# Two operand sums moved ahead of a subtraction, and a 144-column short product, in a two-layer decoder trunk

## The chip, the cores and the metric

The kernel runs on one core of a Trainium2 chip. The metric is the device time of one execution in microseconds; less is better. Five engines work side by side, each through its own queue of instructions: TensorE (PE, with its weight loads PEld), VectorE (DVE), ScalarE (ACT), GpSimd (POOL) and SyncE (SP). Here POOL and SP only start transfers.

## The reference

The program computes two layers of a decoder trunk on 512 tokens of width 1024 in float32. Each layer adds three sub-layers to its input, and each of them is normalised before and after:

```python
for l in range(DEPTH):                     # DEPTH = 2
    h = rms_norm(x, gn[0])
    x = x + 0.5 * rms_norm(swiglu(h, w_ffn1_gate[l], w_ffn1_up[l], w_ffn1_down[l]), gn[1])
    h = rms_norm(x, gn[2])
    ...                                    # recurrence, windowed attention, two gated branches
    x = x + rms_norm(mixed @ w_out[l], gn[3])
    h = rms_norm(x, gn[4])
    x = x + 0.5 * rms_norm(swiglu(h, w_ffn2_gate[l], w_ffn2_up[l], w_ffn2_down[l]), gn[5])
```

`swiglu` is `(silu(h @ w_gate) * (h @ w_up)) @ w_down` with an inner width of 2816, that is 22 blocks of 128 columns. Four of these feed-forward stages and two mixers (the middle sub-layer) make the program.

## The kernel before

**Products from halves.** TensorE multiplies numbers of reduced precision (fp32r). So that the result has the precision of float32, every operand is split into a high half `hi` (a cast) and a low half `lo` (the rest), and `mm3` issues three matmuls for each product of two blocks: hi·hi, hi·lo and lo·hi.

**The stream of weights.** The class `Stream` loads weights from `wall` into tiles `w32` (4 buffers), and `split` turns them into pairs `whi` and `wlo` (6 buffers each). What is split next, and when its instructions are written, is set by `ahead` (line 373), which `used` calls whenever TensorE's instructions for a block have been written. The instructions for TensorE stand in the order in which the program writes them; those for the other engines are placed by a scheduler, except for those that `pin` or `hold` keep in the order of the program.

**A pair of weights.** Most of a feed-forward stage's gate and up products are made by `sevenths` (line 1036), which makes the four quarters of one output block from seven smaller products instead of eight. It takes a pair of weight tiles u and u+1 and needs four stationary operands of it, which `split` makes in the order a, b, c, d:

- a is the tile u itself, d the second half of the tile u+1. Their low halves are made by a transfer: ACT writes −w, rounded, into `wlo` (line 355), ACT casts `whi` (line 359), and POOL starts a DMA that adds w to what stands in `wlo` (line 358).
- b is the sum `t13` (lines 340 and 341, on DVE), c the sum `t`, which takes `t13` further (lines 347 and 348 before the change). Their `whi` is a cast on ACT (line 359), their `wlo` a subtraction on DVE (line 363), which reads that cast.

Between the making of b's sums and its low half stands `self.product()`, which places the last step of the previous output block, the product of gate and up (`gate`, line 1087). That step needs ACT's silu (line 1084), which needs the sums of the seven products (lines 1063, 1065, 1069 and 1070, on DVE). The sums have two buffers (tag `tt`), which the row of gains `grow` (line 733) and the tiles `mv` of the recurrence (line 1183) share.

In one pair TensorE makes 84 matmuls of 256 columns: 7 products of 4 blocks of 3 matmuls. The first feed-forward stage has 15 pairs, the other three have 19 each; each mixer has 4 pairs, and there `split` does not pin its work.

**After the pairs** comes `down` (line 700): the product with `w_down`, in matmuls of 512 columns. Its first part, `both(j, 0)`, takes whole blocks; then `quarters` (line 950) makes seven products from quarters, whose operands (`Late`, line 649; `quarter`, line 258) are made by ACT, DVE and POOL while the first part runs. After the first of the seven products ACT copies two results out (line 978).

**Short products.** `lead` (line 1032) is a matmul of only a few columns into a place that the next matmul overwrites; its result is not used. It stands at the head of the pairs of a stage, with 144 columns, and in `quad` (line 995), where the first products of a stage run over the two halves of the tokens one after the other: ahead of the third product of each half, with 112 columns. Five `quad` calls run in halves, so there are ten of these.

Of the kernel before, what the change touches and what calls it, by code (L numbers as in the profile page):

```python
# [7 lines left out]
F32 = mybir.dt.float32  # L8
# [3 lines left out]
ALU = mybir.AluOpType  # L12
# [3 lines left out]
P = 128  # L16
D = 1024
# [20 lines left out]
TURN = 0  # L38
SEVEN = 16
ASIDE = 16  # L40
LEAD, LEAD_IN = 144, 112
ORDER = ("p1", "p3", "p7", "p2", "p6", "p5")
HEADS = (0, 4, 1, 5, 2, 6, 3, 7)

# [2 lines left out]
def trunk(ctx: ExitStack, tc: tile.TileContext, xin, wall, gains, lbT, hgain, sinks, c_dist, c_mask, c_ident, out):  # L47
    nc = tc.nc
    cp = ctx.enter_context(tc.tile_pool(name="cp", bufs=1))
    sb = ctx.enter_context(tc.tile_pool(name="sb", bufs=1))  # L50
# [9 lines left out]
    def nm(s):  # L60
        seq[0] += 1
        return f"{s}_{seq[0]}"
# [7 lines left out]
    def acc():  # L70
        return ps.tile([P, S], F32, tag="acc", name=nm("acc"), bufs=5)
# [43 lines left out]
    def mm(o, lhsT, rhs, start, stop):  # L115
        nc.tensor.matmul(o, lhsT, rhs, start=start, stop=stop)  # L116
        n = 1
        for d in rhs.shape[1:]:
            n *= d
        if rhs.dtype == F32:  # L120
            order.t += max(n / 2.4, 27.0) * (2 if lhsT.shape[1] == 64 and n < 256 else 4)
        else:
            order.t += max(n / 2.4, 107.0)
# [24 lines left out]
    pin = tc.keep_in_program_order  # L148
# [10 lines left out]
    class Stream:  # L159
# [164 lines left out]
        def split(self):  # L324
            it = self.items[self.done]
            if it.kind[0] == "p":
                return self.quarter(it)
            u, last = it.u, it.kind in "uvd"
            self.load(u + (1 if it.kind in "uv" else 2))
            it.hi, it.lo = (sb.tile([P, D + 64], F32R, tag=t, name=nm(t), bufs=WS)[:, it.at : it.at + D] for t in ("whi", "wlo"))  # L330
            w, h = self.raw[u], (slice(0, D // 2), slice(D // 2, D))
            cols = (slice(0, D),)
            if it.kind == "u" and u < 2:
                cols = h
            if it.kind in "bcd":
                v = self.raw[u + 1]
            if it.kind == "b":

                self.t13 = sb.tile([P, D], F32, tag="tt", name=nm("tt"), bufs=2)
                pin(nc.vector.tensor_tensor(self.t13[:, h[0]], w[:, h[0]], v[:, h[0]], op=ALU.add))  # L340
                pin(nc.vector.tensor_tensor(self.t13[:, h[1]], v[:, h[0]], v[:, h[1]], op=ALU.add))
                w = self.t13
                self.product()
            elif it.kind == "c":

                t = sb.tile([P, D], F32, tag="tt", name=nm("tt"), bufs=2)
                pin(nc.vector.tensor_tensor(t[:, h[0]], self.t13[:, h[0]], v[:, h[1]], op=ALU.add))
                pin(nc.vector.tensor_tensor(t[:, h[1]], t[:, h[0]], w[:, h[1]], op=ALU.add))  # L348
                w = t
            elif it.kind == "d":  # L350
                w = v
                cols = h[1:]
            for c in cols:
                if it.kind in "vad":
                    i = nc.scalar.mul(it.lo[:, c], w[:, c], -1.0)  # L355
                    if self.pinned or self.tight:
                        pin(i)
                    nc.gpsimd.dma_start(it.lo[:, c].bitcast(F32), w[:, c], accum_op=ALU.add)  # L358
                i = nc.scalar.copy(it.hi[:, c], w[:, c])  # L359
                if u < 6 or self.pinned or self.tight:  # L360
                    pin(i)
                if it.kind not in "vad":
                    self.hold(nc.vector.tensor_tensor(it.lo[:, c], w[:, c], it.hi[:, c].bitcast(F32), op=ALU.subtract))  # L363
            self.done += 1
            self.flight += 1
            if last:
                nu = u + (1 if it.kind in "uv" else 2)
                for i in range(u, nu):
                    self.raw.pop(i)
                    self.freed += 1  # L370
                self.load(self.freed + W32)
# [46 lines left out]
    def wmm(o, b, mv, start, stop, poll=True):  # L418

        mm3(o, b[2:], mv, start, stop)  # L420
        ws.used(b)
        if poll:
            order.poll()

    def cut(pair, c):
        return pair[0][:, c], pair[1][:, c]
# [73 lines left out]
    def pair_split(v, how=split):  # L500
        return how(v, to=(big(F32R, [P, 2, S // 2]), big(F32R, [P, 2, S // 2])))
# [13 lines left out]
    class First(Quarters):  # L515
# [44 lines left out]
        def sums(self):  # L560

            k = len(self.x56)
            a = []
            for i in range(2):
                f = xs[k + 4 * i]
                nc.vector.scalar_tensor_tensor(f, f, g_sb[:, 0, 0, k + 4 * i : k + 4 * i + 1], self.rb, op0=ALU.mult, op1=ALU.mult)
                a.append([f[:, c] for c in HALF])
            self.x124.append([])
            for v in (a[0][0], a[1][0], a[1][1]):
                x = big(F32R, [P, 2, S // 2])  # L570
                split(v, to=(x[:, 0, :], x[:, 1, :]))
                self.x124[k].append(x)
            for x, v in zip((self.x56, self.x37), quarter_sums(a[0][0], a[1][0], a[0][1], a[1][1])):
                x.append(pair_split(v))
# [74 lines left out]
    class Late:  # L649
# [20 lines left out]
        def first(self, k):  # L670
            x = big(F32R, [P, 2, S // 2])
            self.x1.append(split(self.src[k][:, HALF[0]], to=(x[:, 0, :], x[:, 1, :]), hold=pin))
# [322 lines left out]
    def quad(pre, halves):  # L995

        o = [acc() for _ in range(4)]
        blocks = {}
        ws.pinned = halves
        for half in (0, 1) if halves else (None,):  # L1000
            c = WHOLE if half is None else HALF[half]
            for k in range(KT):
                order.until(lambda: pre.have[half or 0] > k)
                for j in range(4):
                    if (k, j) not in blocks:
                        blocks[k, j] = ws.next(uses=2 if halves else 1)
                    if halves and (k, j) == (0, 2):
                        lead(o[j][:, c], blocks[k, j][2], pre.h[k][0][:, c], LEAD_IN)
                    wmm(o[j][:, c], blocks[k, j], cut(pre.h[k], c), k == 0, k == KT - 1)
            ws.pinned = False  # L1010
        return o
# [20 lines left out]
    def lead(o, st, mv, n):  # L1032

        mm(o[:, :n], st, mv[:, :n], True, True)
# [60 lines left out]
    def ffn(l, n, pre, nxt, halves=True):  # L1095
        a = []

        def gated(og, ou):
            z, u = big(), big()
            if first:  # L1100
                pin(nc.vector.tensor_tensor(z, og, pre.rb, op=ALU.mult))
                nc.scalar.activation(out=z, in_=z, func=AF.Silu)
                nc.vector.tensor_tensor(u, ou, pre.rb, op=ALU.mult)
                nc.vector.tensor_tensor(u, u, z, op=ALU.mult)
            else:
                nc.scalar.activation(out=z, in_=og, func=AF.Silu)
                pin(nc.vector.tensor_tensor(u, ou, z, op=ALU.mult))
            a.append(u)

        first = isinstance(pre, First)  # L1110
        o = quad(pre, halves)
        if first:
            o.append(project(pre))
            o.append(project(pre, aux))
            order.until(lambda: pre.rb is not None)
        if not first:
            pre.sums()
            pre.sums()
        for j in range(2):
            gated(o[2 * j], o[2 * j + 1])  # L1120
        if first:
            gated(o[4], o[5])
            for j in range(3, FIRST):
                if j > 3:
                    order.until(lambda: pre.laid)
                    pre.sums()
                if j == 4:
                    pre.sums()
                if j == FIRST - 1:
                    ws.most = AHEAD + 2  # L1130
                gated(project(pre), project(pre))
            fast(pre, a, FIRST)
        else:
            pre.sums()
            ws.most = AHEAD + 2
            og = project(pre)
            pre.sums()
            gated(og, project(pre))
            fast(pre, a, 3)
        return down(a, FT, l, n + 1, nxt, True)  # L1140
# [125 lines left out]
    def mixer(l, pre, nxt):  # L1266
# [40 lines left out]
        def run(i, heads):  # L1307
# [8 lines left out]
            for n in range(2):  # L1316
                order.spawn(outputs(i + n, box[n]), n * WAIT["apart"])

        o = quad(pre, True)
        order.spawn(run(0, [head(o[2 * i], o[2 * i + 1], i) for i in range(2)]))  # L1320

# [176 lines left out]
    pre = First()  # L1498
# [68 lines left out]
    for l in range(DEPTH):  # L1567
        pre = ffn(l, 0, pre, (l, 2), halves=l > 0)
        pre = mixer(l, pre, (l, 4))
        pre = ffn(l, 4, pre, (l + 1, 0) if l + 1 < DEPTH else None)  # L1570
# [81 lines left out]
```

## Time and profile before

| what | value |
|---|---|
| time, median of 3 runs | 2051.83 us (2051.58 to 2052.47) |
| span of the profiled execution | 2051.3 us |
| PE busy | 2032.0 us |
| DVE busy | 1623.7 us |
| ACT busy | 1249.4 us |
| POOL busy | 268.3 us |
| read from and written to memory | 213.43 MB and 14.73 MB |

The profiled execution is one execution; its span, from the first to the last instruction, is 0.5 us under the median of the times. A share of busy time is an average over stages. Matmuls are pipelined, so PE counts as busy from a matmul's start to its modelled end, and two neighbours overlap; how fast they follow each other is read from their starts, or from their number in a window.

### The profile page before, as it was taken

Reading aid. Unit: us, or ns where it says so; the run is one execution under the profiler, and the core shown is the slowest. Engines: PE = TensorE matmul, PEld = TensorE weight load, DVE = VectorE, ACT = ScalarE, POOL = GpSimd, SP = SyncE. Lnnn points to the kernel's source line nnn. Section 1 sums busy time; section 2 is a strip of 40 time slices with the busy share of each in tenths; the row PEclk is TensorE's granted clock in tenths of the full one; section 3 lists DMA queues with packets and bytes.
Section 4 is the critical chain, followed back from the end, with each engine's and each line's share of the span. In section 5 each row is a group of like instructions: output and inputs, shape, how many; then the busy total and the mean of one; then the engine's idle time right before and its main releaser. Section 6 shows DMA issues by size and latency. Waiting matters only on the chain. (4 is left out here: it accounts for less than half of the span.)

```text
span 2051.3 us, 36423 instructions
## 1 busy us (share of the span) xinstructions
PE 2032.0 (99%) x13553; PEld 1815.3 (88%) x13553; DVE 1623.7 (79%) x2894; ACT 1249.4 (61%) x2213; POOL 268.3 (13%) x318
## 2 busy tenths in 40 slices
PE   9999999999999999999999999999999999999998
PEld 8899878877888999997899998888778989999987
DVE  5887889767676778888988878987686858788888
ACT  7556687446355556657866566874554545665684
POOL 0111140000000011113201111400000100111140
PEclk9999999999999999999999999999999999999999
DMA  8577788312237357778757778872122553777694
GB/s 257 152 194 186 189 187 238 117 65 70 73 94 215 113 146 192 190 188 205 200 157 191 193 186 203 179 230 92 62 73 62 137 194 102 182 190 194 175 201 123
DMA packets 166801, 328.07 MB, mean 160 GB/s; under 512 B 19072, under 2 KB 85088, under 8 KB 166624
## 3 DMA queue, kind: packets, MB, share of 16 engines
q1 hardware_dynamic: 122416, 228.16, 33.5%
q0 software_dynamic: 44064, 97.54, 27.3%
q8 instruction: 106, 1.74, 0.4%
q14 instruction: 71, 0.58, 0.1%
q10 hardware_dynamic: 144, 0.05, 0.0%
HBM read 213.43 MB, written 14.73 MB: 111 GB/s over the span
## 5 line engine op out<-in xcount | busy, mean ns | idle before, releaser
L116 PE MATMUL acc<-s,whi 128*128 128x256 f32 (+1 forms) x4998 | 1023.7, 304 | 0.3 <-ACT whi L359 0.3
L116 PEld LDWEIGHTS acc<-s,whi 128*128 128x128 f32 x4998 | 793.6, 188 | 47.0 <-issue 3.2
L116 PE MATMUL acc<-s,wlo 128*128 128x256 f32 (+1 forms) x2488 | 755.3, 304 | 5.3 <-DMA wlo<-w 5.2
L116 PEld LDWEIGHTS acc<-s,wlo 128*128 128x128 f32 x2488 | 467.9, 188 | 30.6 <-DMA wlo<-w 7.4
L116 PE MATMUL acc<-whi,s 128*128 128x512 f32 x1360 | 443.9, 394 | 4.9 <-ACT whi L288 3.6
L359 ACT CAST whi<-w 128x1024 fp32r<-128x1024 f32 (+1 forms) x310 | 284.8, 926 | 144.9 <-PE acc L116 103.5
L359 ACT CAST whi<-tt 128x1024 fp32r<-128x1024 f32 x160 | 168.1, 1051 | 250.5 <-DVE tt L348 192.3
L358 POOL DMA_DIRECT2D wlo<-w x178 | 154.7, 870 | 1232.8 <-ACT wlo L355 987.0
L116 PEld LDWEIGHTS acc<-whi,s 128*128 128x128 f32 x1360 | 255.8, 188 | 64.3 <-ACT whi L288 4.8
L363 DVE TENSOR_TENSOR wlo<-tt,whi 128x1024 fp32r<-128x1024 f32 x160 | 196.1, 1225 | 131.4 <-ACT whi L359 129.1
L116 PE MATMUL acc<-wlo,s 128*128 128x512 f32 x680 | 267.3, 393 | 1.8 <-DVE wlo L296 1.6
L116 PE MATMUL aux<-s,whi 128*128 128x256 f32 (+1 forms) x1296 | 228.5, 279 | 0.0
L363 DVE TENSOR_TENSOR wlo<-w,whi 128x1024 fp32r<-128x1024 f32 (+1 forms) x132 | 157.4, 1206 | 74.2 <-ACT whi L359 73.9
L116 PEld LDWEIGHTS aux<-s,whi 128*128 128x128 f32 x1296 | 196.6, 188 | 1.1 <-issue 0.5
L116 PE MATMUL aux<-s,wlo 128*128 128x256 f32 (+1 forms) x648 | 180.4, 278 | 0.0
L116 PEld LDWEIGHTS acc<-wlo,s 128*128 128x128 f32 x680 | 128.2, 188 | 32.1 <-DVE wlo L296 7.5
L355 ACT ACTIVATE wlo<-w 128x1024 fp32r<-128x1024 f32 (+1 forms) x178 | 153.1, 862 | 2.6 <-DMA w<-wall 1.9
L116 PE MATMUL aux<-whi,s 128*128 128x512 f32 x432 | 143.9, 390 | 0.0
L444 POOL DMA_DIRECT2D s<-s x128 | 111.1, 972 | 219.1 <-ACT s L432 100.2
L116 PEld LDWEIGHTS aux<-s,wlo 128*128 128x128 f32 x648 | 121.7, 188 | 0.3
L296 DVE TENSOR_TENSOR wlo<-s,whi 128x512 fp32r<-128x512 f32 x160 | 102.7, 686 | 9.9 <-ACT whi L288 8.1
L432 ACT CAST s<-s 128x512 fp32r<-128x512 f32 (+1 forms) x140 | 70.8, 548 | 44.8 <-DVE s L491 39.3
(184 smaller groups left out, 2466.9 us busy)
## 6 DMA issues: line engine op xcount, KB each, us to landing
w<-wall SPq DMA_DIRECT2D x267, 512.0 KB, 3.7
wlo<-w POOLq DMA_DIRECT2D x98, 512.0 KB, 5.1
w<-wall SPq DMA_DIRECT2D x224, 128.0 KB, 3.5
wlo<-w POOLq DMA_DIRECT2D x80, 256.0 KB, 3.3
s<-wall SPq DMA_DIRECT2D x128, 128.0 KB, 4.3
s<-s POOLq DMA_DIRECT2D x64, 256.0 KB, 5.0
x_d<-s SPq DMA_DIRECT2D x48, 256.0 KB, 4.6
s<-x_d SPq DMA_DIRECT2D x48, 256.0 KB, 5.1
```

Source lines behind the costliest of these rows:

```text
L116: nc.tensor.matmul(o, lhsT, rhs, start=start, stop=stop)
L296: pin(nc.vector.tensor_tensor(it.lo[:, h[c]], w[c], it.hi[:, h[c]].bitcast(F32), op=ALU.subtract))
L355: i = nc.scalar.mul(it.lo[:, c], w[:, c], -1.0)
L358: nc.gpsimd.dma_start(it.lo[:, c].bitcast(F32), w[:, c], accum_op=ALU.add)
L359: i = nc.scalar.copy(it.hi[:, c], w[:, c])
L363: self.hold(nc.vector.tensor_tensor(it.lo[:, c], w[:, c], it.hi[:, c].bitcast(F32), op=ALU.subtract))
L432: (hold or ws.hold)(nc.scalar.copy(hi, src))
L444: nc.gpsimd.dma_start(lo.bitcast(F32), src, accum_op=ALU.add)
```

## The change

Two things change. In `split`, the sum `t`, the operand of c, is made in the step of b: its first half directly after `t13`, then `self.product()`, then its second half, all ahead of b's low half. The step of c only takes the finished tile. The same instructions are issued, in another order. In `quad`, the short product has 112 columns in the first half of the tokens, as before, and 144 in the second.

```diff
-LEAD, LEAD_IN = 144, 112
+LEAD, LEAD_IN = 144, (112, 144)
...
                 pin(nc.vector.tensor_tensor(self.t13[:, h[0]], w[:, h[0]], v[:, h[0]], op=ALU.add))
                 pin(nc.vector.tensor_tensor(self.t13[:, h[1]], v[:, h[0]], v[:, h[1]], op=ALU.add))
+                self.t = t = sb.tile([P, D], F32, tag="tt", name=nm("tt"), bufs=2)
+                pin(nc.vector.tensor_tensor(t[:, h[0]], self.t13[:, h[0]], v[:, h[1]], op=ALU.add))
+                self.product()
+                pin(nc.vector.tensor_tensor(t[:, h[1]], t[:, h[0]], w[:, h[1]], op=ALU.add))
                 w = self.t13
-                self.product()
             elif it.kind == "c":
 
-                t = sb.tile([P, D], F32, tag="tt", name=nm("tt"), bufs=2)
-                pin(nc.vector.tensor_tensor(t[:, h[0]], self.t13[:, h[0]], v[:, h[1]], op=ALU.add))
-                pin(nc.vector.tensor_tensor(t[:, h[1]], t[:, h[0]], w[:, h[1]], op=ALU.add))
-                w = t
+                w = self.t
...
-                        lead(o[j][:, c], blocks[k, j][2], pre.h[k][0][:, c], LEAD_IN)
+                        lead(o[j][:, c], blocks[k, j][2], pre.h[k][0][:, c], LEAD_IN[half])
```

The first place is DVE in a pair of a feed-forward stage. In the rows before, `tt_1049` is `t13` and `tt_1082` is `t`; the two rows that write `wlo` are the low halves of b and of c.

```order
L1070 TENSOR_TENSOR m_1002<-aux_921,s_923 128x512
L340 TENSOR_TENSOR tt_1049<-w_175_847,w_176_849 128x512
L341 TENSOR_TENSOR tt_1049<-w_176_849 128x512
L1087 SCALAR_TENSOR_TENSOR s_1036<-m_1002 128x512
L363 TENSOR_TENSOR wlo_1048<-tt_1049,whi_1047 128x1024
L347 TENSOR_TENSOR tt_1082<-tt_1049,w_176_849 128x512
L348 TENSOR_TENSOR tt_1082<-tt_1082,w_175_847 128x512
L363 TENSOR_TENSOR wlo_1081<-tt_1082,whi_1080 128x1024
L1063 TENSOR_TENSOR m_1129<-acc_1039,s_1042 128x2x256
```

The same place after the change, where `tt_1052` is `t`, and its two sums have the lines 343 and 345.

```order
L1070 TENSOR_TENSOR m_1002<-aux_924,s_926 128x512
L340 TENSOR_TENSOR tt_1049<-w_175_847,w_176_849 128x512
L341 TENSOR_TENSOR tt_1049<-w_176_849 128x512
L343 TENSOR_TENSOR tt_1052<-tt_1049,w_176_849 128x512
L1087 SCALAR_TENSOR_TENSOR s_1036<-m_1002 128x512
L345 TENSOR_TENSOR tt_1052<-tt_1052,w_175_847 128x512
L363 TENSOR_TENSOR wlo_1048<-tt_1049,whi_1047 128x1024
L363 TENSOR_TENSOR wlo_1084<-tt_1052,whi_1083 128x1024
L1063 TENSOR_TENSOR m_1129<-acc_1039,s_1042 128x2x256
```

Both sums of `t` now stand ahead of the low half of b, one on each side of the gate product (line 1087), and the two low halves stand side by side. ACT's order within such a pair is the same before and after.

The second place is ACT ahead of the first pair of the first mixer, where nothing is pinned. Before, `whi_6429` is c of the first pair, `whi_6463` its d, `whi_6516` and `wlo_6517` are a of the second pair, and `whi_6485` is a weight of a branch.

```order
L432 CAST s_6399<-s_6393 128x512
L432 CAST s_6403<-s_6394 128x512
L432 CAST s_6419<-aux_6414 128x512
L1439 ACTIVATE s_6448<-acc_6407 128x512
L1051 COPY s_6479<-acc_6475 128x256
L359 CAST whi_6429<-tt_6431 128x1024
L359 CAST whi_6463<-w_1083_6087 128x512
L355 ACTIVATE wlo_6464<-w_1083_6087 128x512
L359 CAST whi_6485<-w_1096_6157 128x1024
L359 CAST whi_6516<-w_1118_6239 128x1024
L355 ACTIVATE wlo_6517<-w_1118_6239 128x1024
```

After the change c of the first pair is `whi_6432`; the other names of weights are the same.

```order
L359 CAST whi_6432<-tt_6362 128x1024
L359 CAST whi_6463<-w_1083_6087 128x512
L359 CAST whi_6485<-w_1096_6157 128x1024
L355 ACTIVATE wlo_6464<-w_1083_6087 128x512
L359 CAST whi_6516<-w_1118_6239 128x1024
L432 CAST s_6402<-s_6396 128x512
L355 ACTIVATE wlo_6517<-w_1118_6239 128x1024
L432 CAST s_6406<-s_6397 128x512
L359 CAST whi_6545<-tt_6547 128x1024
L432 CAST s_6422<-aux_6417 128x512
L1439 ACTIVATE s_6448<-acc_6410 128x512
L1051 COPY s_6479<-acc_6475 128x256
```

The work on the weights has moved ahead of the splits of the activations (line 432), of the gate of a branch (line 1439) and of the copy of the first product (line 1051).

On PE only the five short products in the second half change, from 128x112 to 128x144; every other row stands where it stood. On SP the load of the row of gains (line 734) stands one load of weights later in four of its six places, and POOL's order is the same.

## The prediction

> **What bounds the kernel now.** I read the page first, then the waits of PE, then where those waits lie.
>
> ```profile
> PE 2032.0 (99%) x13553; PEld 1815.3 (88%) x13553; DVE 1623.7 (79%) x2894; ACT 1249.4 (61%) x2213; POOL 268.3 (13%) x318
> PE acc L116 <- DMA wlo<-w: 5.2, 8, 1.2
> PE acc L116 <- ACT whi L288: 3.6, 3, 1.6
> ```
>
> PE sets the end. Its two largest waits, for low halves that come by DMA and for high halves in `down`, make 8.8 us, 0.4% of the span. If that were all, little could be won. But a busy PE need not run at its best, so I look at lengths: for the four feed-forward stages in order, the short product that opens the pairs, the first matmul of 512 columns after them, and the copy of the first of the seven products in `down`. The columns are start, duration, instruction.
>
> ```profile
> 88.20 0.51 PE L116 MATMUL acc<-s,whi 128*128 128x144 f32 x3
> 231.12 0.40 PE L116 MATMUL acc<-whi,s 128*128 128x512 f32 x1
> 265.74 1.05 ACT L978 COPY s<-acc 128x512 f32<-128x512 f32 x2
> ...
> 728.74 0.39 PE L116 MATMUL acc<-s,whi 128*128 128x144 f32 x2
> 913.55 0.40 PE L116 MATMUL acc<-whi,s 128*128 128x512 f32 x1
> 947.25 1.06 ACT L978 COPY s<-acc 128x512 f32<-128x512 f32 x2
> ...
> 1062.97 0.51 PE L116 MATMUL acc<-s,whi 128*128 128x144 f32 x3
> 1246.28 0.40 PE L116 MATMUL acc<-whi,s 128*128 128x512 f32 x1
> 1281.47 1.05 ACT L978 COPY s<-acc 128x512 f32<-128x512 f32 x2
> ...
> 1742.11 0.39 PE L116 MATMUL acc<-s,whi 128*128 128x144 f32 x2
> 1929.76 0.40 PE L116 MATMUL acc<-whi,s 128*128 128x512 f32 x1
> 1960.57 1.06 ACT L978 COPY s<-acc 128x512 f32<-128x512 f32 x2
> ```
>
> The first stage takes 231.12 − 88.20 = 142.92 us for 15 pairs, 9.53 us each. The others have 19 pairs, and at that pace would take 181.03. They take 184.81, 183.31 and 187.65: 3.8, 2.3 and 6.6 us more. From the end of the pairs to the copy the four stages take 34.62, 33.70, 35.19 and 30.81 us for the same instructions: the last is 3.8, 2.9 and 4.4 us quicker than the others.
>
> Next, what runs beside PE in a pair: DVE from one L1063 to the next, ACT, and PE's wait there. The bracket holds the idle time before an instruction and what ended it.
>
> ```profile
> 1114.15 0.68 DVE L1063 TENSOR_TENSOR m<-acc,s 128x512 f32<-128x512 f32 x1
> ...
> 1117.13 0.68 DVE L341 TENSOR_TENSOR tt<-w 128x512 f32<-128x512 f32 x1
> 1117.73 0.68 DVE L1087 SCALAR_TENSOR_TENSOR s<-m 128x512 f32<-128x512 f32 x1
> 1118.99 1.23 DVE L363 TENSOR_TENSOR wlo<-tt,whi 128x1024 fp32r<-128x1024 f32 x1 [0.57 <-ACT whi L359]
> 1120.13 0.69 DVE L347 TENSOR_TENSOR tt<-tt,w 128x512 f32<-128x512 f32 x1
> 1120.85 0.69 DVE L348 TENSOR_TENSOR tt<-tt,w 128x512 f32<-128x512 f32 x1
> 1122.71 1.23 DVE L363 TENSOR_TENSOR wlo<-tt,whi 128x1024 fp32r<-128x1024 f32 x1 [1.17 <-ACT whi L359]
> 1123.85 0.69 DVE L1063 TENSOR_TENSOR m<-acc,s 128x512 f32<-128x512 f32 x1
> 1117.90 1.05 ACT L359 CAST whi<-tt 128x1024 fp32r<-128x1024 f32 x1 [0.56 <-DVE tt L341]
> 1121.63 1.05 ACT L359 CAST whi<-tt 128x1024 fp32r<-128x1024 f32 x1 [2.41 <-DVE tt L348]
> 1122.58 0.63 ACT L355 ACTIVATE wlo<-w 128x512 fp32r<-128x512 f32 x1
> 1121.40 0.38 PE L116 MATMUL acc<-s,wlo 128*128 128x256 f32 x1 [0.80 <-DMA wlo<-w]
> ```
>
> DVE's period is 1123.85 − 1114.15 = 9.70 us, more than the 9.53 of PE, and L1063 waits for nothing: DVE and ACT hand work to each other in a loop slower than PE. DVE is late for want of a partner, since 0.57 + 1.17 = 1.74 us of its period are waits for ACT, while ACT waits 2.41 for L348. Behind that cast stand the −w of d and a and their transfers. So each pair loses 0.17 us of lead, 3.2 over 19 pairs; late in a stage PE waits for a transfer, and enters `down` with DVE and ACT behind. The last stage is the control: its PE takes 187.65 / 19 = 9.88 us a pair, longer than the loop, so the loop gained lead, and its `down` is the quick one.
>
> Why was PE slow there? The window rows give length, then PE's busy time with its number of matmuls, PEld, DVE, ACT and POOL, the granted clock and DMA.
>
> ```profile
> 1063.00:1120.00 57.00, 57.00 (x505) 57.00 (x504) 45.23 (x64) 35.10 (x49) 10.33 (x12) 1.00 0.76 183
> 1772.00:1929.00 157.00, 157.00 (x1335) 157.00 (x1335) 127.04 (x177) 97.71 (x134) 26.66 (x31) 1.00 0.77 192
> 1771.60 0.39 PE L116 MATMUL acc<-s,wlo 128*128 128x256 f32 x1 [0.41 <-DMA wlo<-w]
> ```
>
> 57.00 / 505 is 112.9 ns a matmul, 157.00 / 1335 is 117.6, with the clock at 1.00 in both. PE has two paces for the same matmuls; the slow one began at the one wait of that stage and held to its end.
>
> **The sums of c ahead of b's low half.** Nothing is added or taken away in instructions; two DVE sums of 0.72 us (from one start to the next) move ahead of a subtraction of 1.14. After L341 DVE goes on for 0.72 + 0.60 + 0.72 us (L343, L1087, L345), to 1119.77, which covers b's cast on ACT (1117.90 to 1118.95). c's cast runs while DVE makes b's low half. Both waits, 1.74 us, lose their cause, and the loop becomes 9.70 − 1.74 = 7.96 us. ACT's busy share, 35.10 / 57.00, gives 5.97 us a pair; with DVE at 7.96 and PE at 9.53, PE is the slowest, and DVE and ACT will wait for it. c's cast, and all of ACT behind it, starts about 0.1 us after L345's end at 1119.77, that is 1.75 us sooner in each pair until buffers stop it.
>
> Behind the moved sums stands b's low half. It starts at 1119.77 instead of 1118.99, 0.78 later, and ends near 1120.9. PE reads it 24 matmuls after the start of the group whose third matmul is the row of 1121.40: 22 × 0.113 = 2.5 us later, at 1123.9. The delay costs nothing while that cover of 3 us lasts. The gate product, one sum later by 0.72, feeds only `down`.
>
> What this gives, against the profiled execution:
> - Pairs: the three stages fall to the first one's pace, 3.8 + 2.3 + 6.6 = 12.7 us. This counts the waits and the slow pace of the last stage, which needs the wait to begin. Bounds: 12.7, and 6.4 if the last stage stays as slow as it is (1335 matmuls × 4.7 ns = 6.3 us).
> - Entry to `down`: the three slower stages fall to the last one's length, 3.8 + 2.9 + 4.4 = 11.1. Bounds: 11.1, and 0 if DVE's own work there is what is late. I take the upper end because the last stage has the same work and only a better lead.
> - Mixer: unpinned, so its order changes.
>
> ```profile
> 588.22 1.05 ACT L359 CAST whi<-tt 128x1024 fp32r<-128x1024 f32 x1
> 592.10 1.06 ACT L355 ACTIVATE wlo<-w 128x1024 fp32r<-128x1024 f32 x1
> 603.11 0.38 PE L116 MATMUL acc<-s,wlo 128*128 128x256 f32 x1 [1.22 <-DMA wlo<-w]
> ```
>
> The −w of the second pair's a, at 592.10, now stands ahead of four small steps and of c's former place at 588.22. 1.2 us sooner is enough to end the wait of 1.22. Bounds: +1.2, and −1.2 if the steps now behind the casts (line 432) come late for PE; I take 1.2, since no row names PE waiting for line 432 there.
>
> The load of the gains' row stands one load later in SP's queue; it is read only after the seven products, so I cost it at nothing.
>
> One part of the 4.4 us is a clock.
>
> ```profile
> 1272.97 0.50 PE L116 MATMUL acc<-whi,s 128*128 128x512 f32 x1 [1.59 <-ACT whi L288]
> 1274.10:1277.50 3.40, 3.40 (x9) 2.60 (x8) 3.37 (x9) 1.31 (x3) 0.86 (x1) 0.50 1.03 257
> ```
>
> After a wait of 1.59 us the granted clock was 0.50 for 3.40 us, a loss of 1.7. I count it as going with the wait. The Trainium skill (TensorE: Matmul & The Clock Gate, "What's actually happening") says that the clock halves after an idle window of some 3.4 us; by that the wait was too short to be the cause, and the sum would be 1.7 us less. Here the trace speaks against it, as PE was not idle that long.
>
> **The short product.** Five times, 32 more columns: by the pace above 14 ns each, 0.07 us together. What it may move is the pace behind it.
>
> ```profile
> L116 PE MATMUL acc<-s,whi 128*128 128x256 f32 x44 | 7.7, 276 | 0.0
> 360.96 0.51 PE L116 MATMUL acc<-s,whi 128*128 128x112 f32 x3
> L116 PE MATMUL acc<-s,whi 128*128 128x256 f32 x59 | 10.6, 282 | 0.0
> ```
>
> The groups are of 88.6 to 98.6 us, behind the 144 columns at 88.20, and of 361.3 to 371.4, behind the 112 columns of a second half. A matmul's mean is 276 ns at the quick pace and 282 at the slow. If 144 columns bring the quick pace here too, the 59 matmuls of this group and half as many with the low half, 88 × 4.7 ns × 5 = 2.0 us are won; if not, 0.07 lost. The 144 row comes behind 512 columns, not 256, so it is no sure guide: I take the middle, 1.0.
>
> **Sum.** 12.7 + 11.1 + 1.2 + 1.0 = 26.0 us, against the span 2051.3; the median lies 0.5 above the span, so 2051.8 − 26.0 = 2025.8.
>
> **The rivals.**
> 1. *The pace turns.* The waits go, but one stage of pairs runs at 117.6 ns: 19 × 84 × 4.7 ns = 7.5 us, hence about 2033. For it: the last stage shows that a stage can stay slow to its end. Against: the first runs all its 15 pairs quick. Chance 0.19.
> 2. *`down` is late by itself.* Only the pairs, the mixer and the short product give: 2051.8 − 14.9 = 2036.9. Against: the last stage. Chance 0.10.
> 3. *The transfers don't come sooner*, because POOL starts them later as DVE's gaps close; PE still waits for low halves, and the time stays near 2051. Against it:
>
> ```profile
> L358 POOL DMA_DIRECT2D wlo<-w x37 | 31.9, 861 | 162.2 <-ACT wlo L355 160.8 <-ACT whi L359 1.3
> 1123.51 0.86 POOL L358 DMA_DIRECT2D wlo<-w  x1 [6.71 <-ACT wlo L355]
> ```
>
> The start at 1123.51 ran beside the L363 of 1122.71 and took 0.86, like the mean of 37. The Trainium skill (GPSIMD Engine Reference, "Specifications") says that GpSimd contends with VectorE's instructions of two SBUF inputs, which all these sums are; the row shows none. Chance 0.04.
> 4. *Slower: the loop gets longer.* L1087 now stands between the sums of c and waits for ACT's silu; were silu late, L345, c's cast and, through ACT's queue, the next silu would all be late. It decides from a period of 9.70 us, that is when new waits exceed the 1.74 removed; at 10.0 it costs 0.3 × 72 pairs = 22 us, 2073. Against: L341 and L343 give ACT 1.3 us for a silu that now makes L1087 wait for nothing. Chance 0.03.
>
> The forecast has 0.64. The range 2021 to 2037 holds it and rivals 1 and 2. Its lower end is the whole 2.0 of the short product and some 4 us of PE's smaller waits, which a better lead may end: of the 19.3 us between span and PE's busy time 10.5 are left beside the 8.8 above. Differences under 0.2% (4.1 us) can't be told from none: faster 0.93 (the forecast, 1 and 2), same 0.04 (3), slower 0.03 (4).
>
> **What would show it.** Right: the two L363 of a pair side by side with hardly a wait; L1063 or L1070 waiting for PE; no PE wait for `wlo` in the pairs; 181 us from short product to 512 columns in the three stages; about 31 us from there to the copy in all four; 276 ns in the second halves. Wrong: a stage with 281 ns, a `down` still over 33 us to the copy, or L363 still behind ACT.

## The result, and the profile after

| what | before | after |
|---|---|---|
| time, median of 4 runs | 2052.15 us (2051.58 to 2052.83) | 2024.78 us (2024.60 to 2024.90) |
| span of the profiled execution | 2051.3 us | 2023.0 us |

The ratio is 0.9868, with a 95% interval from 0.9854 to 0.9882: faster by 1.3%. The forecast was 2025.8. The medians differ by 27.4 us and the spans by 28.3; the profiled execution after took 2024.79 us. From the page of the changed kernel, the busy times; then its waits of PE, with the total, the number and the longest.

```profile
PE 2016.2 (100%) x13553; PEld 1809.1 (89%) x13553; DVE 1624.3 (80%) x2894; ACT 1265.2 (63%) x2213; POOL 268.3 (13%) x318
```

```profile
PE aux L116 <- DVE eps_t L139: 1.1, 1, 1.1
PE acc L126 <- DVE s L863: 1.0, 2, 0.5
PE acc L116 <- DVE wlo L296: 0.2, 1, 0.2
```

The waits for `wlo` by DMA (5.2 us) and for `whi` of L288 (3.6) are gone; three small ones are left, and PE is busy for 2016.2 of 2023.0 us. The three landmarks of each stage, as before: the short product, the first matmul of 512 columns, the first copy in `down`.

```profile
88.27 0.51 PE L116 MATMUL acc<-s,whi 128*128 128x144 f32 x3
231.19 0.40 PE L116 MATMUL acc<-whi,s 128*128 128x512 f32 x1
261.31 1.06 ACT L978 COPY s<-acc 128x512 f32<-128x512 f32 x2
...
722.02 0.51 PE L116 MATMUL acc<-s,whi 128*128 128x144 f32 x3
903.02 0.40 PE L116 MATMUL acc<-whi,s 128*128 128x512 f32 x1
933.15 1.05 ACT L978 COPY s<-acc 128x512 f32<-128x512 f32 x2
...
1048.93 0.51 PE L116 MATMUL acc<-s,whi 128*128 128x144 f32 x3
1229.93 0.40 PE L116 MATMUL acc<-whi,s 128*128 128x512 f32 x1
1260.05 1.06 ACT L978 COPY s<-acc 128x512 f32<-128x512 f32 x2
...
1720.81 0.39 PE L116 MATMUL acc<-s,whi 128*128 128x144 f32 x2
1901.81 0.40 PE L116 MATMUL acc<-whi,s 128*128 128x512 f32 x1
1931.93 1.06 ACT L978 COPY s<-acc 128x512 f32<-128x512 f32 x2
```

The differences account for most of the gain in the span:

| stretch | stage 1 | stage 2 | stage 3 | stage 4 | won |
|---|---|---|---|---|---|
| pairs, before | 142.92 | 184.81 | 183.31 | 187.65 | |
| pairs, after | 142.92 | 181.00 | 181.00 | 181.00 | 12.8 |
| from there to the copy, before | 34.62 | 33.70 | 35.19 | 30.81 | |
| from there to the copy, after | 30.12 | 30.13 | 30.12 | 30.12 | 13.8 |

That is 26.6 of the 28.3 us. From the first stage's copy to the second stage's pairs, where the first mixer lies, it is 463.00 before and 460.71 after, 2.3 us less; the other stretches differ by 0.1 to 0.3 us, and their sum is 0.6 us longer.

A pair after the change, on DVE, from one pair of low halves (L363, two in one row) to the next; the bracket holds the idle time and what ended it.

```profile
1109.99 2.48 DVE L363 TENSOR_TENSOR wlo<-tt,whi 128x1024 fp32r<-128x1024 f32 x2
1113.17 0.69 DVE L1063 TENSOR_TENSOR m<-acc,s 128x512 f32<-128x512 f32 x1 [0.70 <-PE acc L116]
...
1115.89 0.69 DVE L1070 TENSOR_TENSOR m<-aux,s 128x512 f32<-128x512 f32 x1 [0.85 <-PE aux L116]
...
1117.70 0.69 DVE L343 TENSOR_TENSOR tt<-tt,w 128x512 f32<-128x512 f32 x1
1118.30 0.69 DVE L1087 SCALAR_TENSOR_TENSOR s<-m 128x512 f32<-128x512 f32 x1
1118.90 0.69 DVE L345 TENSOR_TENSOR tt<-tt,w 128x512 f32<-128x512 f32 x1
1119.51 2.48 DVE L363 TENSOR_TENSOR wlo<-tt,whi 128x1024 fp32r<-128x1024 f32 x2
```

The two low halves stand side by side and neither waits for ACT. DVE's period is 9.52 us, and 0.70 + 0.85 = 1.55 of it are waits for PE, where before it waited 1.74 for ACT. By these brackets DVE itself needs 9.52 − 1.55 = 7.97. L1087, now between the sums, waits for nothing here. Over all pairs the pages tell the same; before, then after, with the idle time behind the second bar:

```profile
L363 DVE TENSOR_TENSOR wlo<-tt,whi 128x1024 fp32r<-128x1024 f32 x160 | 196.1, 1225 | 131.4 <-ACT whi L359 129.1
L363 DVE TENSOR_TENSOR wlo<-tt,whi 128x1024 fp32r<-128x1024 f32 x160 | 195.4, 1221 | 9.9 <-ACT whi L359 7.3
```

ACT beside the pair after the change:

```profile
1110.16 1.05 ACT L359 CAST whi<-tt 128x1024 fp32r<-128x1024 f32 x1 [0.49 <-DVE tt L345]
1111.81 0.63 ACT L355 ACTIVATE wlo<-w 128x512 fp32r<-128x512 f32 x1 [0.60 <-PE acc L116]
1114.53 1.06 ACT L355 ACTIVATE wlo<-w 128x1024 fp32r<-128x1024 f32 x1 [1.58 <-PE aux L116]
```

The cast of c waits 0.49 us for its sum where it waited 2.41, and the two −w (L355) wait until PE has let go of a buffer. So the loop is ahead of PE as far as the buffers allow.

### The profile page after: what moved, and what is told of

It reads as the page before. It is cut to its first block, busy times and chain, and to the rows that moved or that the text cites. A ratio compares the mean times of both kernels' runs of the same rounds, so it can differ in the third digit from the quotient of the medians.

```text
span 2023.0 us, 36425 instructions
## 1 busy us (share of the span) xinstructions
PE 2016.2 (100%) x13553; PEld 1809.1 (89%) x13553; DVE 1624.3 (80%) x2894; ACT 1265.2 (63%) x2213; POOL 268.3 (13%) x318
## 3 DMA queue, kind: packets, MB, share of 16 engines
q8 instruction: 106, 1.74, 0.3%
## 4 chain that ended last, share of the span: by engine, by line
PE 93%; DVE 3%; ACT 1%; DMA 1%; issue 1%; SPq 0%; DVEq 0%; ACTq 0%
PE acc L116 71%; PE aux L116 20%; PE aux L126 2%; DVE wlo L296 1%; DVE s L264 1%; DMA w<-wall 1%; PE acc L126 0%; ACT whi L288 0%; DVE s L968 0%; SPq L244 0%; ACT s L442 0%; ACT s L443 0%; DVE wlo L363 0%; DVE s L863 0%; DVE s L433 0%
## 5 line engine op out<-in xcount | busy, mean ns | idle before, releaser
L355 ACT ACTIVATE wlo<-w 128x1024 fp32r<-128x1024 f32 (+1 forms) x178 | 154.6, 869 | 137.1 <-PE aux L116 98.2
L363 DVE TENSOR_TENSOR wlo<-w,whi 128x1024 fp32r<-128x1024 f32 (+1 forms) x132 | 157.4, 1205 | 78.3 <-ACT whi L359 78.1
L363 DVE TENSOR_TENSOR wlo<-tt,whi 128x1024 fp32r<-128x1024 f32 x160 | 195.4, 1221 | 9.9 <-ACT whi L359 7.3
L1070 DVE TENSOR_TENSOR m<-aux,s 128x512 f32<-128x512 f32 x80 | 55.2, 690 | 52.0 <-PE aux L116 51.5
```

Source lines behind the costliest of these rows:

```text
L1070: ws.hold(nc.vector.tensor_tensor(m[:, 1:3, :], pairs[2], v[:, ::-1, :], op=ALU.add))
```

## The experiments

The theory: the waits of PE in the pairs and the slow entries to `down` had one cause, a loop of DVE and ACT that was slower than PE; it decides at PE's 9.53 us a pair. The rivals: the gain comes of something else that moved (the short product's pace, the start of c's cast, the place of the gate product), or DVE's own time decides, not its waits.

### The sums alone

The changed kernel with 112 columns in both halves again.

```diff
-LEAD, LEAD_IN = 144, (112, 144)
+LEAD, LEAD_IN = 144, (112, 112)
```

> The changed kernel with 112 columns in both halves, so the sums alone. If the sums made the whole gain, 2024.8 us, within 0.3 of the changed kernel, since the groups of matmuls behind the short product showed 282 ns before and after. If the 144 columns gave part of it, up to 2.0 us more, 2026.8.

2024.57 us (2024.06 to 2024.86), ratio 0.9864 (0.9851 to 0.9878); span 2023.0, and the pairs again 142.92 and three times 181.00. The sums make the whole gain.

### The short product alone

The kernel before with the changed columns.

```diff
-LEAD, LEAD_IN = 144, 112
+LEAD, LEAD_IN = 144, (112, 144)
...
-    lead(o[j][:, c], blocks[k, j][2], pre.h[k][0][:, c], LEAD_IN)
+    lead(o[j][:, c], blocks[k, j][2], pre.h[k][0][:, c], LEAD_IN[half])
```

> The kernel before with 144 columns in the second half, so the short product alone. If it does nothing, 2052.1 us, the time before, within 0.3. If it gave part of the gain, as low as 2050.1; if its 32 more columns cost their length five times, 2052.2.

2052.66 us (2051.43 to 2055.20) against 2052.28 for the kernel before on the same chip, ratio 1.0004 (0.9995 to 1.0013): nothing. Its pairs take 143.29, 184.80, 184.15 and 187.14 us, and PE waits much as before:

```profile
PE acc L116 <- DMA wlo<-w: 3.4, 5, 0.8
PE acc L116 <- ACT whi L288: 2.8, 3, 1.2
```

In the changed kernel, the group of matmuls behind the 144 columns of the first such place, in a window as long as the prediction's behind 112:

```profile
L116 PE MATMUL acc<-s,whi 128*128 128x256 f32 x58 | 10.3, 282 | 0.0
```

282 ns is the slow pace; 144 columns did not turn it. They cost nothing either: from the start of the short product to that of the second matmul behind it, it is 231 ns with 112 columns (52 and 179) and with 144 (69 and 162).

### Only the first half of c's sum ahead

The second half goes back behind b's low half. So c's cast starts 0.57 us sooner in a pair than before, and not 1.75, while b's cast keeps its cover.

```diff
-                pin(nc.vector.tensor_tensor(t[:, h[1]], t[:, h[0]], w[:, h[1]], op=ALU.add))
                 w = self.t13
             elif it.kind == "c":
-                w = self.t
+                t = self.t
+                pin(nc.vector.tensor_tensor(t[:, h[1]], t[:, h[0]], w[:, h[1]], op=ALU.add))
+                w = t
```

> Only the first half of c's sum stands ahead of b's low half; the second half stands behind it as before. By the theory of the loop (DVE and ACT must only be quicker than PE's 9.53 us a pair): L343 and L1087, 1.3 us, still cover b's cast, which removes the wait of 0.57; the loop is 9.70 - 0.57 = 9.13 us, under 9.53, so nearly the whole gain stays, 2025 to 2027 us. By the rival that what counts is how soon c's cast and the transfers behind it start: they start 0.57 us sooner than before instead of 1.75, a third of the gain, about 2043 us.

2025.36 us (2025.24 to 2026.08), ratio 0.9869 (0.9856 to 0.9883). From its DVE, one pair; its lines stand one lower than in the changed kernel.

```profile
1111.05 0.69 DVE L1088 SCALAR_TENSOR_TENSOR s<-m 128x512 f32<-128x512 f32 x1
1111.70 1.23 DVE L364 TENSOR_TENSOR wlo<-tt,whi 128x1024 fp32r<-128x1024 f32 x1
1112.84 0.68 DVE L349 TENSOR_TENSOR tt<-tt,w 128x512 f32<-128x512 f32 x1
1114.70 1.22 DVE L364 TENSOR_TENSOR wlo<-tt,whi 128x1024 fp32r<-128x1024 f32 x1 [1.17 <-ACT whi L360]
...
1120.16 0.69 DVE L1088 SCALAR_TENSOR_TENSOR s<-m 128x512 f32<-128x512 f32 x1
```

The second wait is still there, 1.17 us as before, but the first is gone, and the period is 1120.16 − 1111.05 = 9.11 us, under 9.53. That is enough for all but some 0.8 us of the gain (the sums alone took 2024.57 on the same chip). So it is the loop's length against PE's that counts; the rival by which the gain follows how soon c's cast starts, with 2043 us, is refuted.

### The gate product ahead of both sums

```diff
-                pin(nc.vector.tensor_tensor(t[:, h[0]], self.t13[:, h[0]], v[:, h[1]], op=ALU.add))
                 self.product()
+                pin(nc.vector.tensor_tensor(t[:, h[0]], self.t13[:, h[0]], v[:, h[1]], op=ALU.add))
                 pin(nc.vector.tensor_tensor(t[:, h[1]], t[:, h[0]], w[:, h[1]], op=ALU.add))
```

> Both sums of c ahead of b's low half, but the gate product ahead of both of them instead of between them. If the gate's place is of no account (the silu is ready in time), 2024.8 us. If the gate then waits for silu, by up to 0.3 us a pair, the loop is 8.3 us instead of 8.0, still under 9.53, and the time is again 2024.8; only a wait over 1.5 us a pair would show.

2025.05 us (2024.89 to 2026.80), ratio 0.9869 (0.9855 to 0.9882); pairs of 142.92 and 181.00. The place of L1087 is of no account: it waits for silu at 4 of its 72 places, 3.0 us in all, in either order and in the kernel before.

### More work for DVE in each pair

The second half of c's sum is made three times (two more) or five times (four more), with the same result.

```diff
+                for _ in range(3):
-                pin(nc.vector.tensor_tensor(t[:, h[1]], t[:, h[0]], w[:, h[1]], op=ALU.add))
+                    pin(nc.vector.tensor_tensor(t[:, h[1]], t[:, h[0]], w[:, h[1]], op=ALU.add))
```

Two more:

> The changed kernel with the second half of c's sum made three times instead of once (the same result), so two more DVE instructions of 0.60 us in each pair, ahead of c's cast. Theory of the loop: 7.97 + 2 x 0.60 = 9.18 us of DVE work a pair, under PE's 9.53, so no loss: 2024.8 to 2026 us. Rival, that it counts how soon c's cast and the transfers behind it start: they come 1.2 of the 1.75 us later again, so two thirds of the gain go, about 2043 us.

2024.57 us (2024.46 to 2025.96), ratio 0.9865 (0.9849 to 0.9882). From its DVE, where the loop is still catching up and waits for nothing:

```profile
1107.57 0.69 DVE L1066 TENSOR_TENSOR s<-acc,m 128x512 f32<-128x512 f32 x1
...
1111.64 2.14 DVE L346 TENSOR_TENSOR tt<-tt,w 128x512 f32<-128x512 f32 x3
1113.70 2.49 DVE L364 TENSOR_TENSOR wlo<-tt,whi 128x1024 fp32r<-128x1024 f32 x2
...
1116.82 0.69 DVE L1066 TENSOR_TENSOR s<-acc,m 128x512 f32<-128x512 f32 x1
```

A period of 1116.82 − 1107.57 = 9.25 us costs nothing. It is all DVE's own work. In the kernel before that work was less, some 8 us of the 9.70, and the kernel lost; so what decides is the period with its waits, and not DVE's own time.

Four more:

> The same with four more, five times in all: 7.97 + 4 x 0.60 = 10.4 us a pair, 0.86 over PE's 9.53. Theory of the loop: each stage loses 0.86 us a pair once its lead of some 4.5 us is used up, 8 us in the stage of 15 pairs and 12 in each of the three of 19, and the entries to down are late again, some 17 us: 2070 to 2085 us, slower than the kernel before. Rival, that it counts how soon c's cast starts: 2.4 us later than in the changed kernel, 0.65 later than before the change: about 2062 us.

2121.55 us (two runs, 2121.25 and 2121.86), ratio 1.0336 (1.0315 to 1.0357): over what was expected. Its DVE, without a wait:

```profile
1182.75 0.68 DVE L1064 TENSOR_TENSOR m<-acc,s 128x512 f32<-128x512 f32 x1
...
1187.54 3.59 DVE L346 TENSOR_TENSOR tt<-tt,w 128x512 f32<-128x512 f32 x5
1191.05 2.48 DVE L364 TENSOR_TENSOR wlo<-tt,whi 128x1024 fp32r<-128x1024 f32 x2
1193.44 0.68 DVE L1064 TENSOR_TENSOR m<-acc,s 128x512 f32<-128x512 f32 x1
```

and its waits of PE:

```profile
PE acc L116 <- DVE wlo L364: 20.4, 40, 0.7
PE acc L116 <- DMA wlo<-w: 15.3, 24, 1.6
```

The side was right, the size wrong, for two reasons. A repeat costs 0.72 us and not the 0.60 of a lone sum: five take 1191.05 − 1187.54 = 3.51, one takes 0.61 in the changed kernel, and (3.51 − 0.61) / 4 = 0.72. So the period is 1193.44 − 1182.75 = 10.69. And the pairs, at 156.69, 203.45, 203.85 and 204.37 us, give 82.4 us of the 96.5 between the two profiled spans. Of the other 14, 13.0 lie between the end of the pairs and the first copy in `down`: that takes 33.43, 33.82, 33.39 and 32.86 us in the four stages, where it takes 30.12 in the changed kernel, so the entries are late again. Together with the run with two more sums this brackets the threshold: 9.25 us a pair is free, 10.69 is not, nor is the 9.70 of the kernel before, and PE's 9.53 lies between.

### The size of the short product

Two variants of the changed kernel, run once each, look for what sets PE's pace. In the first, the five second halves have 96, 128, 160, 192 and 256 columns:

```diff
-LEAD, LEAD_IN = 144, (112, 144)
+LEAD, LEAD_IN = 144, [112, 96, 112, 128, 112, 160, 112, 192, 112, 256]
...
-    lead(o[j][:, c], blocks[k, j][2], pre.h[k][0][:, c], LEAD_IN[half])
+    lead(o[j][:, c], blocks[k, j][2], pre.h[k][0][:, c], next(sizes))
```

> The changed kernel with 96, 128, 160, 192 and 256 columns in the second half of the five places in turn, 112 in the first halves. If a size shifts the matmuls behind it to the quick pace, their mean is 276 ns there instead of 282, and the stage is 0.4 us shorter. If the pace does not depend on it, 282 ns at all five. Time within 2 us of 2024.8.

2024.09 us. The windows of 9.6 us behind the five places, in that order:

```profile
356.60:366.20 9.60, 9.60 (x87) 9.60 (x86) 3.68 (x3) 4.47 (x5) 0.00 (x0) 1.00 0.37 124
701.20:710.80 9.60, 9.60 (x84) 9.60 (x83) 8.65 (x15) 5.15 (x6) 0.86 (x1) 1.00 0.33 60
1028.00:1037.60 9.60, 9.60 (x84) 9.60 (x83) 8.90 (x15) 5.25 (x6) 0.86 (x1) 1.00 0.31 65
1355.20:1364.80 9.60, 9.60 (x88) 9.60 (x87) 3.68 (x3) 4.61 (x5) 0.00 (x0) 1.00 0.37 123
1700.10:1709.70 9.60, 9.60 (x83) 9.60 (x83) 7.96 (x14) 5.19 (x7) 0.86 (x1) 1.00 0.34 65
```

The first number with an x counts PE's matmuls in the window: 87 and 88 behind 96 and 192 columns, 83 or 84 behind the others. Two sizes turn the pace, but the quick places here also have little DVE work beside them (3.68 us against about 8), so place and size are mixed.

In the second run, the heads of the four stages' pairs have 112, 128, 176 and 208 columns in place of 144:

> The changed kernel with 112, 128, 176 and 208 columns instead of 144 at the head of the pairs of the four feed-forward stages. If the pace of a stage is set by how the short product leaves the matmuls behind it, some stage runs all its pairs at 282 ns and is 5.9 us (15 pairs) or 7.5 us (19 pairs) longer, without any wait; then the slow pace of the last stage before the change came from the phase its wait left, not from the wait itself. If the pace needs a wait, 276 ns in all four and 2024.8 us.

2025.37 us. From its second and last stage:

```profile
724.00:900.00 176.00, 176.00 (x1556) 176.00 (x1555) 146.47 (x206) 114.25 (x153) 30.10 (x35) 1.00 0.80 191
1722.00:1900.00 178.00, 178.00 (x1573) 178.00 (x1572) 148.38 (x210) 115.76 (x154) 30.12 (x35) 1.00 0.79 189
```

176.00 / 1556 and 178.00 / 1573 are 113.1 and 113.2 ns, with 128 and 208 columns; the pairs of the stages with 112 and 176 take 142.92 and 181.01 us. All are quick: at the head of the pairs these sizes make no difference.

### 96 and 192 columns in all five second halves

```diff
-LEAD, LEAD_IN = 144, (112, 144)
+LEAD, LEAD_IN = 144, (112, 96)
```

and the same with 192.

> The changed kernel with 96 columns in place of 144 in all five second halves. Theory that 96 turns the pace wherever it stands: the 88 matmuls behind each of the five are quick, and at the 0.38 us that the one quick place with 96 columns gave, 5 x 0.38 = 1.9 us less than the changed kernel, some 2022.9. Theory that place and not size decides: only the first place is quick, 0.4 us less, 2024.4. The mean of the matmuls behind each of the five places, 276 or 282 ns, tells it.

> As the run with 96 columns, with 192 columns in all five second halves. Theory that 192 turns the pace wherever it stands: five quick places, 1.9 us less, and 5 x 48 columns more cost nothing, since the next matmul started 231 ns after the short product's predecessor for 112 and 144 alike: some 2022.9. Theory of the place: only the fourth is quick, some 2024.4.

2022.68 us (2022.44 to 2023.29) with 96, 2022.92 (2022.31 to 2023.74) with 192, against 2051.70 for the kernel before on the same chip: ratios 0.9857 (0.9843 to 0.9872) and 0.9858 (0.9841 to 0.9874). The spans are 2020.9 and 2021.5. The first and the last place with 96, the last with DVE work beside it:

```profile
356.30:366.20 9.90, 9.90 (x90) 9.90 (x89) 3.68 (x3) 4.72 (x5) 0.00 (x0) 1.00 0.37 124
1698.40:1708.30 9.90, 9.90 (x90) 9.90 (x89) 8.43 (x15) 5.16 (x6) 0.86 (x1) 1.00 0.30 58
```

and the last place in the changed kernel, with 144:

```profile
1699.60:1709.50 9.90, 9.90 (x86) 9.90 (x86) 8.96 (x15) 5.16 (x6) 0.86 (x1) 1.00 0.31 58
```

90 matmuls against 86 in 9.9 us, with much and with little DVE work: among the five second halves the size decides, not the place. From the start of the short product to the end of its group of 256 columns each of the five places takes 10.33 us, with 96 and with 192, where it takes 10.71 in the changed kernel, and 5 × 0.38 = 1.9. So 1.9 us were expected; 2024.78 − 2022.68 = 2.1 and 2024.78 − 2022.92 = 1.9 came, the runs of either lying wholly under those of the changed kernel (on another chip, whose kernel before took 2052.15). These two are the quickest kernels here, and their times don't tell them apart.

## Why the prediction was right

**The loop.** Predicted 7.96 us a pair once its 1.74 us of waits are gone; by the same brackets it is 7.97, and the waits are for PE. This is shown: a loop of 9.11 or 9.25 keeps the gain, one of 10.69 turns it into a loss. The size is a little off all the same. The runs with more sums, which show no wait, give 9.25 − 2 × 0.72 = 10.69 − 4 × 0.72 = 7.81: an instruction on DVE starts before the one ahead of it ends, so a bracket is less than the delay. And L343, L1087 and L345 take 0.60 us each (1117.70 to 1119.51), not 0.72, 0.60 and 0.72. Against 9.53 neither matters.

**Pairs, 12.7.** Measured 12.8. (Against the run with the short product alone, a second execution with the old order of the sums, it is 13.5.) That includes the last stage, whose window now has 157.00 / 1384 = 113.4 ns a matmul where it had 117.6.

```profile
1720.00:1877.00 157.00, 157.00 (x1384) 156.85 (x1383) 132.29 (x189) 101.21 (x133) 27.52 (x32) 1.00 0.80 186
```

In every kernel here whose pairs have no wait, they ran quick from end to end; in the one with the short product alone the last stage was slow again, at 187.14 us. There the slow pace began at a matmul (1769.71) that started 0.19 us after its neighbour, only 0.07 late. That in the pairs the slow pace needs a delay to begin is borne out; why only some delays bring it is open. It is no rule for other places: in the second halves the same pace stands behind a short product, where no wait is listed.

**Entry to `down`, 11.1.** Measured 13.8, the term that was mis-sized. The cause was right, a `down` entered with a late loop. But I took the last stage's 30.81 us as the floor, and that stage was itself late by 0.69: all four now take 30.12, and 4 × 0.69 = 2.8 is the difference. In the run with the short product alone the four take 34.22, 33.70, 34.34 and 31.29 us, 13.1 over 30.12, so this term does not hang on one execution.

**The half clock, 1.7 within that term.** The third stage's entry gave 35.19 − 30.12 = 5.1 us. The stretch where the clock was 0.50, up to the matmuls into `aux` behind it, is now the first row; the second is that stretch in the run with the short product alone, behind the same wait for `whi`, there 1.18 us long.

```profile
1253.76:1257.16 3.40, 3.40 (x17) 2.81 (x16) 2.53 (x7) 1.56 (x4) 0.86 (x1) 1.00 1.05 279
1272.60:1276.00 3.40, 2.73 (x12) 1.93 (x11) 3.37 (x9) 1.31 (x3) 0.86 (x1) 1.00 1.02 251
```

The granted clock is 1.00 in both. So the half clock was gone with the wait, but it need not come with one: with a wait of 1.18 us the clock stayed, and that entry still took 34.34 us. That the 1.59 us brought it is not shown. By the rule of the Trainium skill (TensorE: Matmul & The Clock Gate, "What's actually happening") the wait of 1.59 us was too short to bring the half clock, and its 1.7 us would have stayed; here it did not stay. As the half clock stood at one place in one execution, that doesn't decide against the rule.

**Mixer, 1.2.** The 2.3 us of that stretch are 1.5 at the row of 603.11, whose wait is gone, and 0.8 earlier, in the rest of the first `down`, where small waits for low halves went too. I had counted those only in the range. That the change did this is not shown. The run with the short product alone has the old order on ACT, with the −w of the second pair's a at 591.60, 5.84 us behind the short product of 585.76 (before: 592.10 − 586.27 = 5.83); yet PE has no listed wait in this stretch, and it takes 460.55 us, as short as the 460.71 after. The −w does stand sooner after the change, at 582.50 − 581.06 = 1.44 us behind its short product, but the wait of 1.22 was, as far as two executions tell, one of the profiled execution alone. That something like 1.2 was won here is luck.

**Short product, 1.0.** Measured nothing, with an end of −0.07 and one of 2.0. The middle was no value that could occur: the pace either turns or it does not. 144 does not turn it; 96 and 192 do, and bring the 2.0.

**Span and time.** I took the time to lie 0.5 us over the span. In all executions that have both numbers, of either kernel, it lies 1.7 to 1.9 over it (2051.70 and 2049.9 in one of before, 2024.79 and 2023.0 after), so the profiled execution of before, with its span of 2051.3, was some 1.3 us slower than the median, and part of what I summed was its own, in the mixer's stretch above all. The errors, 2.7 and 1.1 more won in `down` and the mixer's stretch, 1.0 less at the short product, 0.6 lost in the rest and 1.3 around the span, nearly cancel. That 2025.8 is nearer than its terms is luck.

**The rivals.** (1) No stage turned slow. (2) `down` is not late by itself: 30.12 in all four stages. (3) The transfers do come sooner; a start of POOL still takes 0.86 us beside DVE's subtraction of two inputs (the one at 1056.87 lies wholly within the L363 of 1056.54 to 1057.76), so the contention that the Trainium skill states (GPSIMD Engine Reference, "Specifications") is not seen at this place. (4) L1087 waits for silu no more than before, 3.0 us in all, and taking it out from between the sums changes nothing; but the mechanism by which the rival priced a loss, a longer loop, is real, as the run with four more sums shows.

## What to carry to other kernels

When two engines hand work to each other in a loop, compare the loop's period, its waits included, with the bound engine's: where it is longer, a wait that no view counts as costly is what the bound engine pays later, at the next change of stage most of all. Reordering one side so that its partner always has work under way can remove those waits without one instruction less, and repeating a cheap instruction shows how much room is then left. And take as a floor what a stage needs when nothing is late, not the quickest stage that the trace happens to hold. A second trace of the old order tells which waits belong to the kernel and which to one execution.

## What the runs showed of the hardware

- The same 256-column matmuls follow each other at 113 ns or at 118 ns at a granted clock of 1.00. In the pairs the slow pace began at a delay, of 0.41 us in the kernel before, and held for 1335 matmuls.
- A short product ahead of them can set the pace too. In the second halves 96 and 192 columns gave the quick pace at all five places, 112 and 144 the slow one at all five; 128, 160 and 256, at one place each, gave the slow one. In the first halves 112 gave the quick one, and so did 112, 128, 144, 176 and 208 at the head of the pairs. What in the size and the place does it is open.
- 32 more columns in a short product took no time: the start of the next matmul but one stood 231 ns behind its start with 112 and with 144 columns, 229 with 96 and 228 with 192.
- A DVE sum of 128x512 starts 0.60 us after the one before it (1118.30 to 1118.90 above), 0.72 if it reads or rewrites what that one wrote (1120.13 to 1120.85 in the kernel before, and the repeats).
